# Down projection by seven half-size products instead of four quarter blocks, with operand sums made on chip

## The chip, the cores and the metric

One core of a Trainium2 chip runs the kernel. The metric is device time in microseconds (us) of one execution. TensorE multiplies, VectorE and ScalarE do elementwise work, POOL (GpSimd) issues some DMAs, SP issues the others.

## The reference, cut to what matters

One encoder layer on 512 tokens of 1024 features in float32. The change lies in the last step, with D_FF = 2816:

```python
h = rmsnorm(x, pre_ffn_w)
f = (silu(h @ w_gate) * (h @ w_up)) @ w_down
x = x + rmsnorm(f, post_ffn_w)
```

Ahead of it stand an input projection, two kinds of attention, gates and an output projection.

## The kernel before

Every float32 product is made of three matmuls. Each operand is split in a high part, which ScalarE writes by a copy into the type that TensorE reads (fp32r), and a low part, which VectorE writes as raw minus high. `mm3` (L216 to L219) issues high times high, high times low, low times high into one PSUM bank. The class `Weights` (L37 to L174) holds the list of weight units in the order of use: `load_to` (L130) issues the loads on SP's queue, five raw buffers ahead, `split_high` (L139, the copy is L147) and `split_low` (L150, the subtraction is L153) prepare a unit. Operands lie in pools: `wp` with 4 double buffers (`place_w`, L197), `up` with 18 and `up2` with 11 buffers of 128x1024.

The start (L425 to L470) is ordered by hand: `stat0` and `scale0` normalise a block of 128 tokens, `to_hT` transposes it and writes its high part on ScalarE (L339) and its low part on VectorE (L340), two weights are split, and `part` issues the first products.

The gate/up stage (L1101 to L1144) runs 20 pairs of weight units. It uses seven products of half-size blocks in place of eight: 84 matmuls of 256 columns a pair. The sums of weight blocks (S) are made on VectorE (L95 to L107), the high parts on ScalarE (L71); some low parts are made by VectorE (L76), others by ScalarE writing the negative of the high part (L73) and a DMA of POOL that adds the raw data to it (L74, "accumulate DMA" below). `ff_out` (L1031) makes the gated product, 11 tiles `F[j]` of 128x1024: two tiles of 128 hidden features, 512 tokens each.

The down projection (L1146 to L1203) walks 22 tiles of 128 hidden features. The product of a tile is 4 token blocks by 2 column halves by 3 matmuls of 512 columns, 528 in all, in eight PSUM banks. `f_split` (L1160) splits `F[j]`, `W.split_to` the weight. Up to tile 16 all eight banks are advanced together:

```python
    for k in range(KO):
        if k % 2 == 0:
            f_split()
        W.split_to(UD[k] + 4)
        for b in range(NB):
            for n in range(2):
                dn_mm(b, n, k)
```

The last six tiles then run block by block, so that a token block's norm (`scaled`, L978: square on ScalarE L982, sum on VectorE L984, power on POOL L319, weighing L987), its scale-and-add (L1200) and its output DMA (L1202) lie under the next block's matmuls. Only the last block's stand free at the end. Within these stages a scheduler sets each engine's order from the written order; engines execute their own queue in order.

## Time and profile before

| | us |
|---|---|
| median of 3 runs (lowest to highest) | 749.67 (747.67 to 749.79) |
| the profiled execution | 748.33 |
| its span in the trace | 746.6 |
| busy: TensorE, VectorE, ScalarE, POOL | 730.4, 481.1, 376.9, 82.5 |
| first and last start of the down projection's matmuls | 619.61, 739.09 |

The span runs from the first to the last event of the trace; the profiled execution's time is 1.7 us longer. Times below are from the span's start. A share of busy time is an average over stages, so it is read by stage.

### The profile page before, as it was taken

The page shows a single profiled execution, that of the slowest core. Times are in us where ns is not written, and L with a number is a line of the kernel's source. Part 1 is how long each engine was busy: PE and PEld are TensorE (multiplying, and loading weights), DVE is VectorE, ACT ScalarE, POOL GpSimd, SP SyncE. Part 2 cuts the span into 40 slices and gives each one's busy share as a digit, 9 for nine tenths or more (in the row PEclk, how much of TensorE's full clock was granted, in tenths as well). Part 3 has the DMA queues.
Part 4 walks back from the last instruction along what each step waited for, and adds up shares of the span by engine and source line. Part 5 has one row for each costly group of instructions (what it writes and reads, how often), then busy time and mean ns, then how long its engine had stood idle before and what let it go on. Part 6 is the DMA issues. An engine that isn't in the chain of part 4 may idle for free. (4 is left out here: it accounts for less than half of the span.)

```text
span 746.6 us, 11240 instructions
## 1 busy us (share of the span) xinstructions
PE 730.4 (98%) x4368; PEld 644.6 (86%) x4368; DVE 481.1 (64%) x840; ACT 376.9 (50%) x612; POOL 82.5 (11%) x129
## 2 busy tenths in 40 slices
PE   8999999999999999999999999999999999999996
PEld 7887888877888888887889999999999998888884
DVE  5625688888876633466467987777788879222333
ACT  6414565666666632453134766666666656212211
POOL 1001011122320000000011111111111110000000
PEclk9999999999999999999999999999999999999999
DMA  9436646343321213263704588878777883443112
GB/s 255 151 101 202 160 131 163 92 107 98 92 67 30 85 58 111 85 225 111 200 36 154 112 191 197 191 183 198 177 174 175 196 224 115 140 169 120 49 43 70
DMA packets 102582, 101.49 MB, mean 136 GB/s; under 512 B 3537, under 2 KB 85473, under 8 KB 102530
## 3 DMA queue, kind: packets, MB, share of 16 engines
q1 hardware_dynamic: 96080, 82.82, 38.5%
q0 software_dynamic: 6448, 17.97, 11.9%
q8 instruction: 34, 0.56, 0.3%
q14 instruction: 18, 0.15, 0.1%
q10 hardware_dynamic: 2, 0.00, 0.0%
HBM read 74.56 MB, written 4.19 MB: 105 GB/s over the span
## 5 line engine op out<-in xcount | busy, mean ns | idle before, releaser
L153 DVE TENSOR_TENSOR w<-raw,w 128x1024 fp32r<-128x1024 f32 x67 | 82.0, 1226 | 83.7 <-ACT w L147 82.6
L147 ACT ACTIVATE w<-raw 128x1024 fp32r<-128x1024 f32 x67 | 70.4, 1053 | 61.9 <-PE b L219 51.9
L217 PE MATMUL mm<-hT,w 128*128 128x512 f32 x256 | 100.8, 394 | 0.3 <-DVE v L393 0.3
L218 PE MATMUL mm<-hT,w 128*128 128x512 f32 x256 | 99.8, 390 | 0.0
L219 PE MATMUL mm<-hT,w 128*128 128x512 f32 x256 | 99.8, 390 | 0.0
L1118 PE MATMUL b<-Tl,w 128*128 128x256 f32 x240 | 66.8, 278 | 0.0
L1116 PE MATMUL b<-Th,w 128*128 128x256 f32 x240 | 66.8, 278 | 0.0
L1119 PE MATMUL b<-Th,w 128*128 128x256 f32 x240 | 66.8, 278 | 0.0
L217 PEld LDWEIGHTS mm<-hT,w 128*128 128x128 f32 x256 | 48.1, 188 | 10.3 <-DVE v L393 0.7
L219 PEld LDWEIGHTS mm<-hT,w 128*128 128x128 f32 x256 | 48.1, 188 | 10.2
L218 PEld LDWEIGHTS mm<-hT,w 128*128 128x128 f32 x256 | 48.1, 188 | 9.2
L217 PE MATMUL b<-w,fh 128*128 128x512 f32 x144 | 56.0, 389 | 0.0
L218 PE MATMUL b<-w,fh 128*128 128x512 f32 x144 | 56.0, 389 | 0.0
L219 PE MATMUL b<-w,fl 128*128 128x512 f32 x144 | 56.0, 389 | 0.0
L74 POOL DMA_DIRECT2D w<-raw x40 | 34.5, 862 | 169.2 <-ACT w L73 131.3
L1119 PE MATMUL b<-Q,w 128*128 128x256 f32 x160 | 44.5, 278 | 1.1 <-DMA w<-raw 1.1
L1119 PEld LDWEIGHTS b<-Th,w 128*128 128x128 f32 x240 | 45.4, 189 | 0.0
L1116 PEld LDWEIGHTS b<-Th,w 128*128 128x128 f32 x240 | 45.3, 189 | 0.0
L1118 PEld LDWEIGHTS b<-Tl,w 128*128 128x128 f32 x240 | 45.3, 189 | 0.0
L1118 PE MATMUL b<-Q,w 128*128 128x256 f32 x160 | 44.3, 277 | 0.0
L1116 PE MATMUL b<-Q,w 128*128 128x256 f32 x160 | 44.3, 277 | 0.0
L982 ACT ACTIVATE junk<-b 128x512 f32<-128x512 f32 x16 | 9.5, 596 | 61.6 <-PE b L219 56.8
(230 smaller groups left out, 1884.7 us busy)
## 6 DMA issues: line engine op xcount, KB each, us to landing
raw<-in_w_in_dram SPq DMA_DIRECT2D x40, 512.0 KB, 4.3
raw<-in_w_gate_dram SPq DMA_DIRECT2D x22, 512.0 KB, 4.5
raw<-in_w_up_dram SPq DMA_DIRECT2D x22, 512.0 KB, 5.1
raw<-in_w_down_dram SPq DMA_DIRECT2D x22, 512.0 KB, 3.4
w<-raw POOLq DMA_DIRECT2D x20, 512.0 KB, 6.5
K<-K SPq DMA_DIRECT2D x24, 256.0 KB, 3.2
w<-raw POOLq DMA_DIRECT2D x20, 256.0 KB, 6.2
x<-in_x_dram SPq DMA_DIRECT2D x8, 512.0 KB, 7.8
```

The costliest lines, as they stand in the source:

```text
L74: nc.gpsimd.dma_start(lo, src, accum_op=ALU.add)
L147: self.nc.scalar.activation(hi, raw, AF.Copy)
L153: (engine or self.nc.vector).tensor_sub(lo, raw, hi.bitcast(F32))
L217: nc.tensor.matmul(bank, sh, mh, start=first, stop=False)
L218: nc.tensor.matmul(bank, sh, ml, start=False, stop=False)
L219: nc.tensor.matmul(bank, sl, mh, start=False, stop=last)
L982: nc.scalar.activation(junk, bs, AF.Square, scale=1.0 / 32.0, accum_out=ss[:, n:n + 1])
L1116: nc.tensor.matmul(bank[c], sh[:, k], th[:, k], start=opens and k == 0, stop=False, **kw)
L1118: nc.tensor.matmul(bank[c], sh[:, k], tl[:, k], start=False, stop=False, **kw)
L1119: nc.tensor.matmul(bank[c], sl[:, k], th[:, k], start=False, stop=k == 3, **kw)
```

## The change

1. The 22 loaded units are now u = (h, j): two tiles of hidden features (j) and one half of the output columns (h). All j run for h = 0 (pass 0), then for h = 1 (pass 1), there in the order 5 to 10, 0 to 4: the gated product's operands of j = 5 to 10 are kept, those of 0 to 4 prepared again.
2. Each unit's block product is made by seven half-size products (P1 to P7) of sums of blocks: S of the gated product, T of the weight. Each has 2 token blocks by 3 matmuls of 256 columns: 42 a unit, 924 in all, into seven banks.
3. New preparation per unit. Weight: ScalarE writes the high part and its negative (768 columns each), POOL issues an accumulate DMA of 384 KB, all two units ahead; VectorE makes T (512 + 256 + 256), ScalarE its high part, VectorE its low part (1024). Gated product (16 times): ScalarE the high part of 768; its low part is VectorE's for even j, and for odd j ScalarE's negative with an accumulate DMA; VectorE makes S (4 x 256), ScalarE its high part, VectorE its low part.
4. At the end of pass 0 the seven banks are combined (ScalarE once, VectorE seven times, L1303 to L1314) while pass 1 begins; squares and weighing of that half follow in unit 11.
5. At the end of pass 1 the last two units' products stand together, P3 and P2 by halves of their token blocks, each followed by combine, squares, power, weighing (L1331) and scale-and-add with its output DMA (`give`, L1336 and L1338).
6. At the start the first weight's high part is written by VectorE, ahead of the first `to_hT`.

The core of the diff (line numbers L1100 and up in the order rows below are those of the changed file; `product` is L1283 to L1290, `combine` L1296 to L1314):

```diff
@@ -131,8 +132,13 @@
         while self.n_dma < min(n, len(self.units)):
             src, shape, _ = self.units[self.n_dma]
             raw = self.raw_pool.tile([128, 1024], F32, tag="raw", name="raw")
-            view = raw.rearrange("p (a b) -> p a b", a=shape[0])
-            self.nc.sync.dma_start(view, src)
+            if len(shape) == 3:
+                view = raw.rearrange("p (a b c) -> p a b c", a=shape[0], b=shape[1])
+                for a in range(shape[0]):
+                    self.nc.sync.dma_start(view[:, a], src[:, a])
+            else:
+                view = raw.rearrange("p (a b) -> p a b", a=shape[0])
+                self.nc.sync.dma_start(view, src)
...
+    ORDER_D = [(0, j) for j in range(KF // 2)]
+    ORDER_D += [(1, j) for j in (*range(KEEP, KF // 2), *range(KEEP))]
+    UD = [W.add(dram(w_down, 256 * j * D + 512 * h,
+                     [[D, 128], [256, 2], [128 * D, 2], [1, 256]]), (2, 2, 256), None)
+          for h, j in ORDER_D]
...
     stat0(1)
+    W.split_high(nc.vector)
     to_hT(hh, 0, hT, ps_s, "s")
     hh = scale0(1)
-    for _ in range(2):
-        W.split_high()
+    W.split_high()
     W.split_low()
...
+        def a0():
+            f = F[j].rearrange("p a t -> p (a t)")
+            st["f"] = f
+            st["lo"] = low_slots(j, turn)
+            hi, lo = U(F32R, [128, 1024], "fh"), st["lo"][0]
+            nc.scalar.activation(hi[:, :768], f[:, :768], AF.Copy)
+            if j % 2:
+                nc.scalar.activation(lo[:, :768], hi[:, :768].bitcast(F32), AF.Copy, scale=-1.0)
+                nc.gpsimd.dma_start(lo[:, :768], f[:, :768], accum_op=ALU.add)
+            else:
+                nc.vector.tensor_sub(lo[:, :768], f[:, :768], hi[:, :768].bitcast(F32))
+            keep(hi, lo, "A12", "A22", "A11")
+        def s1():
+            f = st["f"]
+            a12, a22, a11, a21 = (f[:, 256 * i:256 * i + 256] for i in range(4))
+            S = st["S"] = U(F32, [128, 1024], "S")
+            nc.vector.tensor_add(S[:, 0:256], a21, a22)
+            nc.vector.tensor_sub(S[:, 256:512], S[:, 0:256], a11)
+            nc.vector.tensor_sub(S[:, 512:768], a21, a11)
+            nc.vector.tensor_sub(S[:, 768:], a12, S[:, 256:512])
+        def s2():
+            hi, lo = U(F32R, [128, 1024], "fh"), st["lo"][1]
+            nc.scalar.activation(hi, st["S"], AF.Copy)
+            nc.vector.tensor_sub(lo, st["S"], hi.bitcast(F32))
+            keep(hi, lo, "S1", "S2", "S3", "S4")
+            fop[j] = out
+        return [a0, s1, s2]
...
+        def d0():
+            W.load_to(UD[u] + 1)
+            raw = st["r"] = W.raws.pop(UD[u])
+            if u % 3 == 2:
+                hi, lo = U(F32R, [128, 1024], "dh"), U(F32R, [128, 1024], "dl")
+            else:
+                hi, lo = place_w(16, 1040)
+            nc.scalar.activation(hi[:, :768], raw[:, :768], AF.Copy)
+            nc.scalar.activation(lo[:, :768], hi[:, :768].bitcast(F32), AF.Copy, scale=-1.0)
+            nc.gpsimd.dma_start(lo[:, :768], raw[:, :768], accum_op=ALU.add)
+            keep(hi, lo, "B21", "B11", "B22")
+            W.n_split += 1
+            W.load_to(W.n_split + W.raw_bufs)
...
+        def d1():
+            raw = st["r"]
+            T = st["T"] = U(F32, [128, 1024], "T")
+            b12 = raw[:, 768:].unsqueeze(1).to_broadcast([128, 2, 256])
+            nc.vector.tensor_sub(T[:, :512].rearrange("p (a b) -> p a b", a=2), b12,
+                                 raw[:, 256:768].rearrange("p (a b) -> p a b", a=2))
+            nc.vector.tensor_sub(T[:, 512:768], raw[:, 512:768], T[:, 0:256])
+            nc.vector.tensor_sub(T[:, 768:], raw[:, 0:256], T[:, 512:768])
+        def d2():
+            if u == NU - 1:
+                hi, lo = U(F32R, [128, 1024], "dh"), U(F32R, [128, 1024], "dl")
+            else:
+                hi, lo = place_w(16, 1040)
+            nc.scalar.activation(hi, st["T"], AF.Copy)
+            nc.vector.tensor_sub(lo, st["T"], hi.bitcast(F32))
+            keep(hi, lo, "T1", "T3", "T2", "T4")
+            wop[u] = out
+        return [d0, d1, d2]
...
+    def down_steps(u):
+        if u >= NU:
+            return []
+        h, j = ORDER_D[u]
+        d = dw[u]
+        f = f_steps(j, h) if h == 0 or j < KEEP else []
+        return f[:1] + [d[1], d[2]] + f[1:]
...
-        nxt = steps_of(n + 1)
+        last_pair = n == len(pairs) - 1
+        nxt = [dw[0][0]] + down_steps(0) if last_pair else steps_of(n + 1)
...
+    PRODS = (("P1", "A11", "B11"), ("P6", "S2", "T2"), ("P5", "S1", "T1"), ("P7", "S3", "T3"),
+             ("P4", "A22", "T4"), ("P3", "S4", "B22"), ("P2", "A12", "B21"))
+    PLAIN_LAST = tuple(PRODS[i] for i in (1, 2, 3, 4, 0, 5, 6))
...
+        (ah, al), (bh, bl) = fop[ORDER_D[u][1]][an], wop[u][bn]
+        for i in halves:
+            o, c = banks[nm][:, 256 * i:256 * i + 256], slice(128 * i, 128 * i + 128)
+            nc.tensor.matmul(o, ah[:, c], bh, start=first and i == 0, stop=False,
+                             skip_group_check=True)
+            nc.tensor.matmul(o, ah[:, c], bl, start=False, stop=False, skip_group_check=True)
+            nc.tensor.matmul(o, al[:, c], bh, start=False, stop=last, skip_group_check=True)
...
+    def combine(nm, h, pv, halves=(0, 1)):
+        i = slice(halves[0], halves[-1] + 1)
+        bank = two(banks[nm])[:, i]
+        q = [two(t)[:, i] for t in pv]
+        if nm == "P1":
+            nc.scalar.activation(q[0], bank, AF.Copy)
+        elif nm == "P6":
+            nc.vector.tensor_add(q[1], q[0], bank)
+        elif nm == "P5":
+            nc.vector.tensor_add(q[2], q[1], bank)
+        elif nm == "P7":
+            nc.vector.tensor_add(ysum[1, h][:, i, 256:], q[2], bank)
+            nc.vector.tensor_add(q[3], q[1], bank)
+        elif nm == "P4":
+            nc.vector.tensor_add(ysum[1, h][:, i, :256], q[3], bank)
+        elif nm == "P3":
+            nc.vector.tensor_add(ysum[0, h][:, i, 256:], q[2], bank)
+        else:
+            nc.vector.tensor_add(ysum[0, h][:, i, :256], q[0], bank)
...
+    def give(r, i, h):
+        b = 2 * r + i
+        y, c = ysum[r, h][:, i], slice(512 * h, 512 * h + 512)
+        nc.vector.scalar_tensor_tensor(y, y, ss3[r, i][:, 3:4], x2[b][:, c],
+                                       op0=ALU.mult, op1=ALU.add)
+        nc.sync.dma_start(dram(out, 16 * b * D + 512 * h,
+                               [[D, 16], [64 * D, 8], [1, 512]]), y)
...
+    dw[1][0]()
     x2 = []
...
+    for u in range(NU - 2):
+        h, j = ORDER_D[u]
+        end = u == HALF - 1
+        nxt = down_steps(u + 1) + ([dw[u + 2][0]] if u + 2 < NU else [])
+        if u + 2 < NU:
+            nxt = nxt[-1:] + nxt[:-1]
+        if u == NU - 3:
+            nxt += down_steps(NU - 1)
+        first = u % HALF == 0
+        if end:
+            for r in range(2):
+                ysum[r, 0] = U(F32, [128, 2, 512], "y3", up2)
+            pv = [t for _ in range(2) for t in halves_of(U(F32, [128, 1024], "pv"))]
+        for p in (PRODS if end else PLAIN_LAST):
+            product(u, p, first, end)
+            if end:
+                combine(p[0], 0, pv)
+            if nxt:
+                nxt.pop(0)()
+        for fn in nxt:
+            fn()
+        if end:
+            banks.clear()
+        if u == HALF:
+            pow_ = U(F32, [128, D], "pow", up2)
+            nc.sync.dma_start(pow_, bcast(post_ffn_w, D))
+            for r in range(2):
+                for i in range(2):
+                    squares(r, i, 0)
+            for r in range(2):
+                for i in range(2):
+                    weigh(r, i, 0)
...
+    for p in PRODS[:5]:
+        for u in (NU - 2, NU - 1):
+            product(u, p, False, u == NU - 1)
+        combine(p[0], 1, pv)
+    for i in range(2):
+        squares(1, i, 1)
+        rstd(1, i)
+        weigh(1, i, 1)
+    for i in range(2):
+        for p in PRODS[5:]:
+            for u in (NU - 2, NU - 1):
+                product(u, p, False, u == NU - 1, (i,))
+            combine(p[0], 1, pv, (i,))
+        squares(0, i, 1)
+        rstd(0, i)
+        weigh(0, i, 1)
+        if i == 0:
+            for q in range(2):
+                for h in range(2):
+                    give(1, q, h)
+        for h in range(2):
+            give(0, i, h)
```

VectorE in the down projection. Before, it has two kinds of rows (`fl` and `w` are low parts of the gated product and of a weight):

```order
L153 TENSOR_TENSOR w<-raw,w 128x1024
L1165 TENSOR_TENSOR fl<-f,fh 128x1024 x4
L153 TENSOR_TENSOR w<-raw,w 128x1024 x4
L1165 TENSOR_TENSOR fl<-f,fh 128x1024
L153 TENSOR_TENSOR w<-raw,w 128x1024 x7
```

After, one even unit of pass 0:

```order
L1187 TENSOR_TENSOR T<-raw 128x512
L1138 TENSOR_TENSOR fl<-f,fh 128x768
L1189 TENSOR_TENSOR T<-raw,T 128x256
L1145 TENSOR_TENSOR S<-f 128x256
L1190 TENSOR_TENSOR T<-raw,T 128x256
L1146 TENSOR_TENSOR S<-S,f 128x256
L1147 TENSOR_TENSOR S<-f 128x256
L1148 TENSOR_TENSOR S<-f,S 128x256
L1198 TENSOR_TENSOR w<-T,w 128x1024
L1153 TENSOR_TENSOR fl<-S,fh 128x1024
```

One low part for a weight unit and half of one for the gated product became seven sums and two or three low parts; an odd unit has all but L1138, and in pass 1 units 11 to 16 have only T's rows.

TensorE, the first matmuls of unit 3 (j = 3, odd; `fl_6333` is A's low part made by ScalarE and the accumulate DMA):

```order
L1287 MATMUL b_6359<-w_6394,fh_6474 128x256 [waits Activation_49]
L1289 MATMUL b_6359<-w_6394,fh_6474 128x256 [waits DMASW3_49]
...
L1287 MATMUL b_6310<-w_6494,fh_6514 128x256 [waits Activation_49]
...
L1289 MATMUL b_6310<-w_6494,fh_6514 128x256 [waits DVE_49]
...
L1290 MATMUL b_6349<-w_6494,fl_6333 128x256 [waits DMASW5_49]
L1287 MATMUL b_6349<-w_6494,fh_6474 128x256
```

The wait on DMASW5 is for the accumulate DMA (L1136) of this unit; it and the 29 matmuls behind it are 30 of the unit's 42.

The end, VectorE, before (the last token block), and after from the first half of P3 on (`ss_7135` and `ss_7138` belong to the two halves of the tokens that finish last):

```order
L987 TENSOR_TENSOR y_6971<-b,pow 128x512
L984 TENSOR_SCALAR ss_6972<-ss_6972 128x1
L987 TENSOR_TENSOR y_6971<-b,pow 128x512
L1200 SCALAR_TENSOR_TENSOR y_6971<-y_6971,ss_6972,x_6819 128x512 x2
```

```order
L1314 TENSOR_TENSOR y_7662<-pv,b 128x256
L1336 SCALAR_TENSOR_TENSOR y_7003<-y_7003,ss_7141,x_7442 128x512
L1336 SCALAR_TENSOR_TENSOR y_7663<-y_7663,ss_7141,x_7442 128x512
L1325 TENSOR_SCALAR ss_7135<-ss_7135 128x1
L1331 TENSOR_TENSOR y_7662<-y_7662,pow 128x512
...
L1336 SCALAR_TENSOR_TENSOR y_7662<-y_7662,ss_7135,x_7438 128x512
L1312 TENSOR_TENSOR y_7662<-pv,b 128x256
L1314 TENSOR_TENSOR y_7662<-pv,b 128x256
L1325 TENSOR_SCALAR ss_7138<-ss_7138 128x1
L1331 TENSOR_TENSOR y_7662<-y_7662,pow 128x512
L1336 SCALAR_TENSOR_TENSOR y_7002<-y_7002,ss_7138,x_7440 128x512
```

Five rows for the last block became a row of some 25 for all four, with the second half's combine (the second L1312 and L1314) behind six L1336. On TensorE the second half's first matmul waits for the first half's L1312.

## Rows read from the trace of the kernel before

**Rows 1.** The page, part 1: busy time, share and instructions of each engine.

```profile
PE 730.4 (98%) x4368; PEld 644.6 (86%) x4368; DVE 481.1 (64%) x840; ACT 376.9 (50%) x612; POOL 82.5 (11%) x129
```

**Rows 2.** Windows: stretch, us, busy PE, PEld, DVE, ACT, POOL, clock, DMA, GB/s.

```profile
540.00:560.00 20.00, 19.93 (x173) 19.73 (x172) 15.96 (x25) 13.08 (x18) 3.81 (x5) 1.00 0.77 179
640.00:650.00 10.00, 10.00 (x45) 8.26 (x44) 2.45 (x2) 3.07 (x3) 0.00 (x0) 1.00 0.44 150
```

**Rows 3.** Waits in the down projection: us in total, times, longest.

```profile
ACT w L147 <- PE b L219: 48.6, 13, 4.4
```

**Rows 4.** Timeline of TensorE: start, duration, line; gate/up stage, then down projection.

```profile
594.51 0.28 PE L1116 MATMUL b<-Th,Q 128*128 128x256 f32 x1
...
598.95 0.28 PE L1116 MATMUL b<-Th,w 128*128 128x256 f32 x1
...
619.61 0.40 PE L217 MATMUL b<-w,fh 128*128 128x512 f32 x1
...
739.09 0.39 PE L219 MATMUL b<-whi,fl 128*128 128x512 f32 x1
```

**Rows 5.** Timeline of VectorE in the gate/up stage.

```profile
603.71 0.69 DVE L96 TENSOR_TENSOR S<-S,raw 128x512 f32<-128x512 f32 x1
604.31 0.41 DVE L1124 TENSOR_TENSOR pv<-pv,b 128x256 f32<-128x256 f32 x1
604.64 0.69 DVE L107 TENSOR_TENSOR S<-raw,S 128x512 f32<-128x512 f32 x1
...
605.57 1.22 DVE L76 TENSOR_TENSOR w<-S,w 128x1024 fp32r<-128x1024 f32 x1
606.71 0.41 DVE L1128 TENSOR_TENSOR G<-pv,b 128x256 f32<-128x256 f32 x1
```

**Rows 6.** Timeline of ScalarE in the gate/up stage.

```profile
604.43 1.06 ACT L71 ACTIVATE w<-S 128x1024 fp32r<-128x1024 f32 x1 [2.44 <-DVE S L96]
605.39 1.04 ACT L147 ACTIVATE w<-raw 128x1024 fp32r<-128x1024 f32 x1
...
608.29 0.62 ACT L73 ACTIVATE w<-w 128x512 fp32r<-128x512 f32 x1
608.81 0.37 ACT L1134 ACTIVATE G<-b 128x256 f32<-128x256 f32 x1
```

**Rows 7.** POOL's accumulate DMAs of L74, gate/up stage: instructions, then time to landing.

```profile
L74 POOL DMA_DIRECT2D w<-raw x39: 853/860/872, 419.5 to 609.2; - x39
...
DMA to landing us min/median/max: 4.4/6.4/8.9
```

**Rows 8.** The page, part 5: weight loads of the gate/up stage (busy us, mean ns).

```profile
L1116 PEld LDWEIGHTS b<-Th,w 128*128 128x128 f32 x240 | 45.3, 189 | 0.0
```

**Rows 9.** Timeline of the end, after the last matmul.

```profile
739.57 0.60 ACT L982 ACTIVATE junk<-b 128x512 f32<-128x512 f32 x1 [3.37 <-PE b L219]
...
740.29 0.21 DVE L984 TENSOR_SCALAR ss<-ss 128x1 f32<-128x1 f32 x1 [3.37 <-ACT junk L982]
...
740.65 0.54 POOL L319 TENSOR_TENSOR ss<-ss,mhalf 128x1 f32<-128x1 f32 x1 [7.62 <-DVE ss L984]
741.23 1.42 DVE L1200 SCALAR_TENSOR_TENSOR y<-y,ss,x 128x512 f32<-128x512 f32 x2
```

**Rows 10.** The start: first weight's load, then the timelines of VectorE, ScalarE and TensorE.

```profile
L135 SPq DMA_DIRECT2D raw<-in_w_in_dram x1: 596/596/596, 2.1 to 2.1; - x1
...
DMA to landing us min/median/max: 7.1/7.1/7.1
...
10.81 1.44 DVE L340 TENSOR_TENSOR hT<-tb,hT 128x512 fp32r<-128x512 f32 x2 [1.49 <-ACT hT L339]
...
11.42 2.94 ACT L147 ACTIVATE whi<-raw 128x1024 fp32r<-128x1024 f32 x3
...
12.53 1.20 PE L397 MATMUL mm<-whi,hT 128*128 128x512 f32 x4 [1.63 <-ACT whi L147]
```

**Rows 11.** Windows at the span's end, columns as in rows 2.

```profile
743.00:744.00 1.00, 0.00 (x0) 0.00 (x0) 0.00 (x0) 0.00 (x0) 0.00 (x0) 1.00 0.73 166
744.00:745.00 1.00, 0.00 (x0) 0.00 (x0) 0.00 (x0) 0.00 (x0) 0.00 (x0) 0.76 0.98 348
745.00:746.60 1.60, 0.00 (x0) 0.00 (x0) 0.00 (x0) 0.00 (x0) 0.00 (x0) 0.50 0.02 6
```

More of the change, by code (lines that the diff above doesn't have):

```diff
@@ L26 @@
 UB = 18
+KEEP = 5
 WIN = ((0, 192), (64, 248), (192, 248), (320, 192))
@@ L1089, in block_kernel, with low_slots @@
     ff_out(G, Uu)
+    low = {}
+    def low_slots(j, turn):
+        n = {0: {1: 0, 2: 1, 3: 2, 4: 3, 5: 0, 6: 1, 7: 2, 8: 3},
+             1: {0: 0, 1: 1, 2: 2, 3: 3}}[turn].get(j)
+        if n is None:
+            pool = up if (turn, j) == (0, 0) else up2
+            return U(F32R, [128, 1024], "fl", pool), U(F32R, [128, 1024], "fl", pool)
+        if not low:
+            for q in range(2):
+                low[q] = hp.tile([128, 4160], F32R, tag="hT", name="fl")
+        t, c = low[n // 2], 32 + 2048 * (n % 2)
+        return t[:, c:c + 1024], t[:, c + 1024:c + 2048]
@@ new lines, in block_kernel, with f_steps, keep @@
+    fop, wop = {}, {}
+    def f_steps(j, turn):
+        st, out = {}, {}
+        def keep(hi, lo, *names):
+            for i, nm in enumerate(names):
+                c = slice(256 * i, 256 * i + 256)
+                out[nm] = hi[:, c], lo[:, c]
+        def a0():
[25 more added lines that the diff above has]
+        return [a0, s1, s2]
@@ new lines, in w_steps, with keep @@
+    def w_steps(u):
+        st, out = {}, {}
+        def keep(hi, lo, *names):
+            for i, nm in enumerate(names):
+                c = slice(256 * i, 256 * i + 256)
+                out[nm] = hi[:, c], lo[:, c]
+        def d0():
+            assert W.n_split == UD[u], (W.n_split, UD[u])
+            W.load_to(UD[u] + 1)
[28 more added lines that the diff above has]
+        return [d0, d1, d2]
@@ L1093, in block_kernel @@
+    NU = len(UD)
+    def down_steps(u):
[5 more added lines that the diff above has]
+        return f[:1] + [d[1], d[2]] + f[1:]
+    dw = [w_steps(u) for u in range(NU)]
     ORDER = (("A11", "B11", "A", "p"), ("S2", "T2", "B", "v"), ("S1", "T1", "C", "v5"),
@@ new lines, in block_kernel, with product @@
+    PLAIN_LAST = tuple(PRODS[i] for i in (1, 2, 3, 4, 0, 5, 6))
+    banks = {}
+    ysum, ss3 = {}, {}
+    def product(u, p, first, last, halves=(0, 1)):
+        nm, an, bn = p
+        if nm not in banks:
+            banks[nm] = psB.tile([128, 512], F32, tag="b", name="b")
+        (ah, al), (bh, bl) = fop[ORDER_D[u][1]][an], wop[u][bn]
[5 more added lines that the diff above has]
+            nc.tensor.matmul(o, al[:, c], bh, start=False, stop=last, skip_group_check=True)
@@ new lines, in squares, with rstd @@
+    def squares(r, i, h):
+        if (r, i) not in ss3:
+            ss3[r, i] = sp.tile([128, 4], F32, tag="ss3", name="ss3")
+        junk = U(F32, [128, 512], "junk")
+        nc.scalar.activation(junk, ysum[r, h][:, i], AF.Square, scale=1.0 / 32.0,
+                             accum_out=ss3[r, i][:, h:h + 1])
+    def rstd(r, i):
+        ss = ss3[r, i]
+        nc.vector.tensor_scalar(ss[:, 2:3], ss[:, 0:1], ss[:, 1:2], EPS,
+                                op0=ALU.add, op1=ALU.add)
+        rms_r(ss[:, 2:3], ss[:, 3:4])
@@ new lines, in halves_of @@
+    def halves_of(t):
+        return t[:, :512], t[:, 512:]
+    HALF = KF // 2
+    dw[1][0]()
+    x2 = []
+    for u in range(NU - 2):
[30 more added lines that the diff above has]
+                    weigh(r, i, 0)
+        if u == NU - 6:
+            for b in range(NB):
+                t = U(F32, [128, D], "x2", up2)
+                nc.sync.dma_start(t, x2d[b])
+                x2.append(t)
```

67 lines of the change are left out of this document (10 added, 57 removed).

## The prediction

> **What bounds the kernel now.** I read the page's busy shares first [rows 1]: TensorE is busy for 730.4 of 746.6 us, VectorE for 481.1 and ScalarE for 376.9. So before, the only thing to win is columns streamed on TensorE. Then the busy time by stretches [rows 2], because an average hides that the cover is uneven. In the gate/up stage, which already uses seven products, VectorE is busy 15.96 of 20 us. In the down projection it is busy 2.45 of 10 and ScalarE 3.07, with TensorE at 10.00 of 10. There the preparing engines wait for TensorE, not the other way round [rows 3]: ScalarE's splits waited 48.6 us for matmuls to give buffers back. The question is whether seven products, which put the gate/up stage's kind of load on VectorE, still leave TensorE first.
>
> The prices come from the timelines. In a busy engine I take the step from one start to the next, since the printed duration overlaps the next instruction's start. TensorE [rows 4]: 40 matmuls of 256 columns start from 594.51 to 598.95, so 39 steps of 0.1138. The 528 matmuls of 512 columns start from 619.61 to 739.09: 527 steps of 0.2267, ending at 739.48. VectorE [rows 5]: 0.60 for 512 columns (603.71 to 604.31), 0.33 for 256 (604.31 to 604.64), 1.14 for 1024 (605.57 to 606.71); for 768 I interpolate 0.87. ScalarE [rows 6]: 0.96 for 1024 (604.43 to 605.39), 0.52 for 512 (608.29 to 608.81), 0.74 estimated for 768. When another engine waits for the result I take the duration (1.06, and 0.84 for 768) instead. An accumulate DMA of POOL [rows 7] lands 6.4 us after its issue, 4.4 at best and 8.9 at worst.
>
> **Columns.** 22 units of 42 matmuls are 924 x 0.1138 = 105.2 us; the old stage streamed 528 x 0.2267 = 119.7. Gain **-14.5**. This holds if weight loads stay hidden though their number rises by 396. They do in the gate/up stage: a load takes 0.188 to 0.189 [rows 8] and the matmuls still follow each other at 0.1138. The Trainium skill ("TensorE: Matmul & The Clock Gate", Part 3, The mechanism) says that a load is pulled ahead when its row group does not conflict or it goes to the background buffer; were these full-array loads to conflict, each would stand on the path.
>
> **Pass 0.** VectorE's new work for a unit: sums of weights 0.60 + 0.33 + 0.33 = 1.26, sums of the gated product 4 x 0.33 = 1.32, two low parts of 1024 columns 2.28, together 4.86. Even units also have the low part of 768 columns, 0.87: 5.73. Two units make 10.6, where TensorE needs 2 x 4.78 = 9.56. So VectorE no longer fits beneath TensorE: that alone is 1.0 us per two units. VectorE also stands still when it reaches a low part and ScalarE's copy is not there: the T copy (1.06) starts only when T is complete, and the S copy follows on the same engine, with a 768 copy for the unit two ahead between or after. I work that out at 0.5 us in an odd unit and 0.6 to 1.0 in an even one, about 12.4 us per two units.
>
> The odd units have a longer chain. ScalarE makes the high part and the negative (1.7 us) only after the T copy, a weight copy, the S copy and the weight's negative (1.06 + 0.74 + 1.06 + 0.74), which follow VectorE's T, complete 2.6 us after it starts the even unit. That is about 9.1 us with the waits; then POOL issues the accumulate DMA, landing 6.4 later, and 30 of the unit's 42 matmuls stand behind the first that reads it (3.4 us). Step by step: unit 0 can begin at 620.9, since its S copy waits for sums that stand behind a low part in VectorE's queue, and ends at 625.7. VectorE is through with it at 622.15. Unit 1's accumulate, issued after four ScalarE copies from 620.9, lands at 630.5, so TensorE stands for 4.1 us from 626.35; unit 1 ends at 634.75. Later landings come at 644.6, 656.9, 668.4 and 681.0 for units 3, 5, 7 and 9; unit 9 ends at 684.3 and unit 10 at 689.1. At full rate from 619.6 it would be 672.0, so pass 0 costs **+17.1**. Its lower bound goes by VectorE's busy time alone: from 622.15, 1.47 for the last operations of the gate/up stage in front, 10 units with 52.95, and 1.9 of matmuls behind the last low part is 678.4, so +6.4.
>
> On the accumulate's landing the Trainium skill ("DMA: Bandwidth & Descriptors", Anatomy of one DMA) fits 2.0 us plus the bytes over 436 GB/s for POOL's path: an estimate of 2.9 us for 384 KB, half of what the rows show. By it the odd units would be ready 3.5 us sooner and the sum would come out near 761. The trace decides, since its 6.4 [rows 7] is the same kind of DMA between the same two pools; the bounds are its 4.4 and 8.9, which is -4 to +5 at the two places where a landing counts (the odd units of pass 0 as a constant lag, and unit 20).
>
> **Between the passes.** Seven combines of 0.6 come onto VectorE. Unit 11's T is copied by ScalarE behind the first of them (+0.9) and its low part stands behind another sum and combine (+0.8): **+1.7**, bounds 0 and 2.5. The squares and weighing of pass 0 lie in unit 11, where a unit costs VectorE only 1.26 + 1.14: free, as long as VectorE is not the bound there.
>
> **Pass 1.** For six units only T is new, 2.4 us of VectorE under 4.78 of TensorE: near nothing. The last five units prepare A again: three even, two odd. Unit 20 (j=3) waits for its accumulate until about 740.5, with 70 matmuls of units 20 and 21 behind; small waits before it and S's low part of unit 21 come on top. **+5.8**; without unit 20's wait 2.8.
>
> **The tail.** Before [rows 9]: the last matmul ends at 739.48, ScalarE's square starts at 739.57, VectorE's sum at 740.29, POOL's power at 740.65, and two scale-and-adds at 741.23 end at 742.65: 3.3 us after TensorE's work would be streamed (I take 739.32), then 3.95 for DMA and end. After: the reduced S of unit 21 lets P6, P5 and P7 finish together, so six combines start only then (five of 0.60 and a half one of 0.33, less the 1.0 of matmuls beside them: 2.4 us after the last matmul of the first token half). The second half's products wait for the first half's combine of the same bank, and that half's combine stands in VectorE's queue behind two sums, two weighings, and two, then four scale-and-adds (0.67 each) with another sum and weighing between: 10.6 us after that matmul. Then square, sum, power, weigh and two scale-and-adds as before, 3.3 us. Last VectorE end 13.9 us after that matmul, which is 12.4 after the point where the remaining 12 matmuls (1.4 us) would have streamed out. **+9.1** (12.4 - 3.3); bounds +7 (combines hidden) and +11.
>
> **The start.** The first weight lands 7.1 us after 2.1 [rows 10]. VectorE copies it at about 9.3 to 10.5, before the low part at 10.81. ScalarE's split at 11.42 (three of 2.94, so the first ends near 12.4) held the first real matmul, at 12.53. ScalarE loses one copy and hT's low part, ending at 12.25, becomes the next limit: **-0.7**, bounds -1.0 and +0.3 (VectorE's copy delaying the low part).
>
> **Sum.** -14.5 + 17.1 + 1.7 + 5.8 + 9.1 - 0.7 = +18.5. The profiled execution took 748.33, so 766.8, **767 us**. The median of the runs shown, 749.67, is 1.3 above the profiled one, well inside the range. A change of 0.3%, 2.2 us, is about what a measurement of this kernel tells from none.
>
> **Rivals.** (1) VectorE's busy time alone is the limit: ScalarE's copies and the landings fit beneath. For it: ScalarE's own work for two units, 4 x 0.96 + 7 x 0.74 = 9.0 us, fits beneath VectorE's 10.6. Pass 0 +6.4, boundary +0.9, pass 1 +2.8: -14.5 + 6.4 + 0.9 + 2.8 + 9.1 - 0.7 = +4.0, **752**. Against: queues are in order, and the copies wait for the sums of the same unit.
> (2) Faster: VectorE keeps pace. It decides at 9.56 us for two units. Then pass 0 costs unit 0's 1.2 only, the boundary and pass 1 nothing: -14.5 + 1.2 + 9.1 - 0.7 = -4.9, **743**. For it: VectorE is idle for a fifth of the gate/up stage [rows 2]. Against: 10.6 by the rows, and the order prepares one unit ahead only.
> (3) TensorE's clock falls in the stalls. In the trace the granted clock is still 1.00 up to 744 and 0.50 (1.2 of 2.4 GHz) from 745 [rows 11], and 0.76 in between, so it fell some 5 us after the last matmul. My longest stall is 4.1 us. With two units streamed at half rate, 2 x 4.78 more: +28, **776**.
> (4) The weight loads set the rate: 924 x 0.188 = 173.7 instead of 105.2: **835**. The rows speak against it [rows 4, 8].
>
> **How the numbers follow.** Forecast 0.62 (by its bounds 760 to 773), rival 1 0.17, rival 2 0.05, rival 3 0.14, rival 4 0.02. The range 754 to 778 holds the forecast, most of rival 3 and the upper part of rival 1. Faster by over 0.3%: rival 2, 0.05. Within: the lower end of rival 1, 0.05. Slower: 0.90.
>
> **What would show it.** In the changed profile: matmuls of 0.114 in the down stage; TensorE busy well under 9 of 10 in pass 0, its idle time ended by POOL's accumulate of the gated product or VectorE's low parts; VectorE near 85% there, near half in pass 1; some 17 us from TensorE's first long gap at the end to the span's end; the first real matmul 0.5 to 1 us earlier. The forecast is wrong if pass 0 takes under 60 us (I have 69.5) or the tail's last VectorE operation comes under 9 us after the first half's last matmul.

## The result and the profile after

| | before | after |
|---|---|---|
| median, lowest to highest, us | 749.73 (747.67 to 749.94, 4 runs) | 782.12 (778.36 to 783.13, 4 runs) |
| profiled execution, span, us | 748.33, 746.6 | 783.13, 781.4 |
| mean granted clock of TensorE | 0.999 | 0.973 |

The change makes the kernel 1.0437 times as long, 95% interval 1.0411 to 1.0462: 32 us slower, where 17 were forecast. Slower was right, the size was not, and 782 lies above the range (754 to 778).

The page's busy times of the changed kernel, which answer to [rows 1]:

```profile
PE 743.4 (95%) x4764; PEld 669.6 (86%) x4764; DVE 554.2 (71%) x1001; ACT 434.2 (56%) x685; POOL 109.3 (14%) x158
```

TensorE is busy longer than before though it streams fewer columns, and its share fell. Its timeline (start, duration, line; in brackets the idle time before and what ended it): the down projection's first matmul, the long stalls of pass 0, and the wait near the end.

```profile
625.40 0.38 PE L1287 MATMUL b<-w,fh 128*128 128x256 f32 x1
...
631.41 0.28 PE L1287 MATMUL b<-w,fh 128*128 128x256 f32 x1
634.74 0.58 PE L1290 MATMUL b<-w,fl 128*128 128x256 f32 x1 [3.05 <-DMA fl<-f]
...
651.08 0.58 PE L1290 MATMUL b<-w,fl 128*128 128x256 f32 x1 [1.95 <-DMA fl<-f]
...
667.26 0.58 PE L1290 MATMUL b<-w,fl 128*128 128x256 f32 x1 [3.17 <-DMA fl<-f]
...
691.39 0.58 PE L1290 MATMUL b<-w,fl 128*128 128x256 f32 x1 [1.91 <-DMA fl<-f]
...
766.18 0.55 PE L1287 MATMUL b<-dh,fh 128*128 128x256 f32 x1 [3.03 <-DVE y L1312]
```

Two things stand out. The stage begins at 625.40, where it began at 619.61 before [rows 4]: 5.8 us are lost in code that the change hardly touches. And behind each stall the matmuls take 0.4 to 0.6 us instead of 0.28. The windows (columns as in [rows 2]) show why:

```profile
632.50:633.00 0.50, 0.00 (x0) 0.00 (x0) 0.50 (x1) 0.50 (x1) 0.00 (x0) 1.00 1.12 172
633.00:633.50 0.50, 0.00 (x0) 0.00 (x0) 0.50 (x1) 0.50 (x2) 0.03 (x1) 0.63 0.82 193
633.50:634.00 0.50, 0.00 (x0) 0.00 (x0) 0.50 (x2) 0.42 (x1) 0.50 (x1) 0.50 1.14 305
...
639.50:640.00 0.50, 0.50 (x4) 0.50 (x4) 0.00 (x0) 0.00 (x0) 0.00 (x0) 0.55 0.15 51
640.00:640.50 0.50, 0.50 (x7) 0.50 (x6) 0.00 (x0) 0.00 (x0) 0.00 (x0) 1.00 0.04 14
```

The granted clock falls to 0.50 (1.2 of 2.4 GHz) while TensorE stands, near 633.1, 1.4 us after the last matmul's end at 631.7, and is 1.00 again only near 640, 5 us after the matmuls go on. The other three long stalls of pass 0 have a fall too:

```profile
650.00:650.50 0.50, 0.00 (x0) 0.00 (x0) 0.50 (x3) 0.33 (x1) 0.50 (x1) 0.69 0.76 174
...
667.00:667.50 0.50, 0.24 (x1) 0.24 (x2) 0.50 (x1) 0.50 (x2) 0.00 (x0) 0.76 1.32 147
...
691.00:691.50 0.50, 0.11 (x1) 0.11 (x1) 0.50 (x1) 0.00 (x0) 0.50 (x1) 0.65 1.09 381
```

By the share of 0.50 in each window the falls lie near 650.2, 667.3 and 691.2, which is 1.1, 3.2 and 1.7 us after a last matmul's end. In all, TensorE streams for 17.7 us of pass 0 at half its clock. In the last two windows of the first stall (639.5 to 640.5) VectorE and ScalarE are idle too. What they wait for stands in their timelines:

```profile
640.90 0.85 ACT L1176 ACTIVATE w<-raw 128x768 fp32r<-128x768 f32 x1 [3.57 <-PE b L1290]
641.66 1.04 ACT L1152 ACTIVATE fh<-S 128x1024 fp32r<-128x1024 f32 x1
...
642.73 1.23 DVE L1153 TENSOR_TENSOR fl<-S,fh 128x1024 fp32r<-128x1024 f32 x1 [4.14 <-ACT fh L1152]
```

ScalarE's next weight copy waits for a buffer that the slow matmuls still read; the copy of S stands behind it in ScalarE's queue, and VectorE, the busiest of the preparing engines, waits 4.14 us for that. So a stall slows TensorE, and slow TensorE delays the preparation that ends the next stall.

The end, VectorE, which answers to [rows 9]:

```profile
762.20 0.69 DVE L1303 TENSOR_TENSOR pv<-pv,b 128x512 f32<-128x512 f32 x1 [1.05 <-PE b L1290]
...
765.71 0.41 DVE L1312 TENSOR_TENSOR y<-pv,b 128x256 f32<-128x256 f32 x1
...
773.06 0.41 DVE L1312 TENSOR_TENSOR y<-pv,b 128x256 f32<-128x256 f32 x1
773.39 0.41 DVE L1314 TENSOR_TENSOR y<-pv,b 128x256 f32<-128x256 f32 x1
...
775.91 1.41 DVE L1336 SCALAR_TENSOR_TENSOR y<-y,ss,x 128x512 f32<-128x512 f32 x2 [0.44 <-POOL ss L327]
```

The second half's combine stands 7.4 us behind the first's, as the order said, and the last VectorE instruction ends at 777.3.

### The profile page after: what moved, and what is told of

The parts are those of the page before. It is cut to its first block, busy times and chain, and to the rows that moved or that the text cites. A ratio compares the mean times of both kernels' runs of the same rounds, so it can differ in the third digit from the quotient of the medians.

```text
span 781.4 us, 12448 instructions
## 1 busy us (share of the span) xinstructions
PE 743.4 (95%) x4764; PEld 669.6 (86%) x4764; DVE 554.2 (71%) x1001; ACT 434.2 (56%) x685; POOL 109.3 (14%) x158
## 5 line engine op out<-in xcount | busy, mean ns | idle before, releaser
L223 PE MATMUL mm<-hT,w 128*128 128x512 f32 x256 | 101.9, 398 | 0.3 <-DVE v L401 0.3
L224 PE MATMUL mm<-hT,w 128*128 128x512 f32 x256 | 101.0, 395 | 0.0
L225 PE MATMUL mm<-hT,w 128*128 128x512 f32 x256 | 101.0, 395 | 0.0
L159 DVE TENSOR_TENSOR w<-raw,w 128x1024 fp32r<-128x1024 f32 x49 | 60.0, 1226 | 43.3 <-ACT w L153 43.0
L1290 PE MATMUL b<-w,fl 128*128 128x256 f32 x258 | 70.3, 307 | 10.4 <-DMA fl<-f 10.1
L1287 PE MATMUL b<-w,fh 128*128 128x256 f32 x258 | 70.2, 297 | 2.0 <-ACT fh L1152 1.3
L1289 PE MATMUL b<-w,fh 128*128 128x256 f32 x258 | 70.7, 296 | 0.8 <-DVE w L1198 0.5
L1290 PEld LDWEIGHTS b<-w,fl 128*128 128x128 f32 x258 | 50.8, 213 | 11.4 <-DMA fl<-f 10.9
L153 ACT ACTIVATE w<-raw 128x1024 fp32r<-128x1024 f32 x49 | 51.4, 1052 | 12.6 <-PE mm L405 7.7
L225 PEld LDWEIGHTS mm<-hT,w 128*128 128x128 f32 x256 | 48.0, 187 | 11.7
L1287 PEld LDWEIGHTS b<-w,fh 128*128 128x128 f32 x258 | 50.4, 204 | 3.3 <-ACT fh L1152 2.1
L1289 PEld LDWEIGHTS b<-w,fh 128*128 128x128 f32 x258 | 50.5, 203 | 1.3 <-DVE w L1198 0.7
L1245 PE MATMUL b<-Q,w 128*128 128x256 f32 x160 | 45.1, 282 | 0.6 <-DMA w<-raw 0.6
L1242 PE MATMUL b<-Q,w 128*128 128x256 f32 x160 | 45.2, 283 | 0.0
L1245 PEld LDWEIGHTS b<-Th,w 128*128 128x128 f32 x240 | 45.2, 188 | 0.0
```

The source lines that it names most:

```text
L153: self.nc.scalar.activation(hi, raw, AF.Copy)
L159: (engine or self.nc.vector).tensor_sub(lo, raw, hi.bitcast(F32))
L223: nc.tensor.matmul(bank, sh, mh, start=first, stop=False)
L224: nc.tensor.matmul(bank, sh, ml, start=False, stop=False)
L225: nc.tensor.matmul(bank, sl, mh, start=False, stop=last)
L1242: nc.tensor.matmul(bank[c], sh[:, k], th[:, k], start=opens and k == 0, stop=False, **kw)
```

## The experiments

Theories at the start: **place** (the new kind of small tile grows the statistics pool by 192 bytes per partition, moves the pools behind it, and matmuls that read them go slower), **clock** (as above), **landing** or **VectorE** (what sets the pace of pass 0), **tail**. "Pass 0" below is the time from the down projection's first matmul to the start of pass 0's last combine on VectorE: 80.4 us in the change. The forecast's pass 0 ends earlier, with unit 10's last matmul: 68.2 us there (620.9 to 689.1), 76.2 in the change. The kernel before was run again beside each group of runs. Its medians were 749.8, 747.9 and 748.1 us; ratios are to the one of the same group, and a difference between medians of two groups is uncertain by about 2 us.

**The place alone, on the kernel before.** One unused tile:

```diff
+    sp.tile([128, 4], F32, tag="ss3", name="ss3")
     banks = [psB.tile([128, 512], F32, tag="b", name="b") for _ in range(8)]
```

> The kernel before with nothing added but one unused small tile of a new kind in the pool of small statistics, as the change has one: that pool grows by 192 bytes per partition, and the pools behind it (hT with the transposed operands and Q, up2, the attention's) move from addresses that are a multiple of 128 bytes to ones that leave 64. Theory (place): this alone is what makes the changed kernel reach the down projection 5.8 us late instead of 0.7 early; the first matmul of the down projection starts at 626 (before 619.6), the matmuls of 256 columns that read Q follow each other at 0.118 to 0.119 instead of 0.113, and the time is 6 to 9 us above the kernel before. Rival (start): the earlier start shifts the loads against the work and the middle loses by that; then this kernel is within 1 us of before.

Measured 756.22 us (756.09 to 758.24), ratio 1.0092 (1.0074 to 1.0111). Its timeline of TensorE: a run of 12 matmuls that read Q, and the down projection's first.

```profile
590.96 0.28 PE L1116 MATMUL b<-Th,Q 128*128 128x256 f32 x1
...
592.27 0.28 PE L1119 MATMUL b<-Th,Q 128*128 128x256 f32 x1
...
626.57 0.40 PE L217 MATMUL b<-w,fh 128*128 128x512 f32 x1
```

11 steps in 1.31 us are 0.119 each. The same run in the kernel before takes 1.24 (0.113):

```profile
584.49 0.28 PE L1116 MATMUL b<-Th,Q 128*128 128x256 f32 x1
...
585.73 0.28 PE L1119 MATMUL b<-Th,Q 128*128 128x256 f32 x1
```

The changed kernel shows 1.31 too:

```profile
589.66 0.28 PE L1242 MATMUL b<-Th,Q 128*128 128x256 f32 x1
...
590.97 0.28 PE L1245 MATMUL b<-Th,Q 128*128 128x256 f32 x1
```

The order of the instructions on VectorE, ScalarE and POOL is the same as before, and TensorE's waits ahead of the down projection did not grow (4.1 us against 5.2): a 192-byte move of the pools behind costs 6 to 7 us. Place holds.

**The changed kernel with its pools in the old place.**

```diff
-            ss3[r, i] = sp.tile([128, 4], F32, tag="ss3", name="ss3")
+            ss3[r, i] = sp.tile([128, 4], F32, tag="ss2", name="ss3")
```

> The changed kernel with its statistics tiles of a kind that the pool already has, so that no pool moves; the order of all instructions is the same. Theory (place): the first matmul of the down projection starts at 618 to 619.5 (changed kernel 625.4), and the time is 7 to 11 us below the changed kernel's 782.1, 771 to 775. Rival: 782, as changed.

Measured 772.45 (771.48 to 773.75), ratio 1.0298 (1.0279 to 1.0318): 9.7 us below the change. Its down projection begins at

```profile
617.90 0.38 PE L1287 MATMUL b<-w,fh 128*128 128x256 f32 x1 [0.17 <-ACT fh L1152]
```

7.5 us earlier than in the change; the other 2 lie in the down projection, where pass 0 is 77.2 instead of 80.4. The nine traces of this kernel and its variants below begin the down projection between 617.9 and 620.1, and they are apart by nearly as much already 100 us into the trace. So the place costs 5.3 to 7.5 us ahead of the down projection, and this trace is at the upper end. All further variants of the changed kernel start from this one.

**The start alone, on the kernel before** (`W.split_high(nc.vector)` ahead of the first `to_hT`, one `W.split_high()` less behind it).

> The kernel before with the first weight's high part on VectorE ahead of the first transposes, nothing else. Forecast's step: -0.7 us (bounds -1.0 to +0.3). The changed kernel's trace shows -1.2 at 40 us and only -0.2 left at 240 us: by the theory that the rest was lost to the moved addresses, this kernel keeps -1.0 to -1.3 to the end (748.5). Rival: the start's gain is given back at later waits that do not depend on it (attention waits for ScalarE and VectorE): -0.3 to +0.3. Rival (start): the middle drifts as in the changed kernel: +5.

Measured 747.36 (746.93 to 747.44) beside 749.82 of before, ratio 0.9966 (0.9953 to 0.9979). The down projection begins at

```profile
618.25 0.40 PE L217 MATMUL b<-w,fh 128*128 128x512 f32 x1
```

which is 1.4 us earlier than before (span 745.2 beside 746.6), but traces of one and the same beginning differ by 2.2 us, so the gain rests on the ratio: 0.3%, with an interval clear of 1. Of the two parts that were tried alone, place and start, this is the one that gains, and this kernel is faster than both.

**Whether any move by a multiple of 128 bytes is safe** (b_vec with two more unused tiles, 384 bytes).

> b_vec (747.4) with two unused tiles in the statistics pool: the pools behind it move by 384 bytes per partition, from addresses that leave 128 to ones that leave 0 on division by 256, and stay multiples of 128. Theory (the step of 128 is what matters): within 1 us of b_vec, 746.4 to 748.4, and the matmuls that read Q still follow each other at 0.113. Rival (256, or any move costs): 2 to 7 us away.

Measured 752.56 (752.23 to 753.46), ratio 1.0057 (1.0039 to 1.0075): 5 us slower than b_vec by the medians of two groups, 7 by the ratios. The theory's second half fell. The first product of the down projection:

```profile
623.93 0.40 PE L219 MATMUL b<-w,fh 128*128 128x512 f32 x1
```

Here the runs of Th with Q take 1.25 us as before; other pairs of operands lost. By the mean step between starts, Q with w takes 0.118 instead of 0.115, and hT with w (512 columns) 0.233 instead of 0.228. So it isn't a pool's own address on a grid of 128 bytes; that it is the position of the two operands to each other would fit all three kernels, but was not tried by itself.

**The clock.** In the odd units of pass 0, filling matmuls into an unused bank ahead of the one that waits:

```diff
+            if u < 10 and u % 2 and nm == "P4" and i == 0:
+                if "idle" not in banks:
+                    banks["idle"] = psB.tile([128, 512], F32, tag="b", name="idle")
+                for _ in range(FILLS):
+                    nc.tensor.matmul(banks["idle"][:, :256], ah[:, c], bh, start=True, stop=True,
+                                     skip_group_check=True)
```

> As a_place, and 30 matmuls of 256 columns into an unused bank stand on TensorE's queue ahead of the matmul that waits for the accumulate DMA, in units 1, 3, 5, 7 and 9 of pass 0: they fill the stalls (3.4 us each) without touching the results. Theory (clock): in pass 0 the granted clock fell to 0.50 in or behind four stalls of 2.5 to 3.5 us, and the slow stretches hold buffers that ScalarE waits for; with the stalls filled the clock stays at 1.00 in pass 0 and the time is 6 to 10 us below a_place, although 150 matmuls are added. Rival: preparation is the limit all the same and the clock costs nothing: within 2 us of a_place, or up to 10 above it where the filling is longer than the stall.

> As a_fill (769.6) with 20 filling matmuls instead of 30 in each odd unit of pass 0. With 30, TensorE was busy in 5.00 of 5 us throughout pass 0, so 84 + 30 matmuls at 0.114 = 13.0 us set the pace of two units and not the preparation. Theory: with 20 the pace is the preparation's, 12.4 by the forecast, or 104 x 0.114 = 11.8 if that is longer: 3 us shorter in pass 0, 766 to 767.5. Rival: preparation takes 13 us for two units by itself; then stalls of about 1 us come back and the time stays at 769 to 770, or rises if the clock falls.

With 30: 769.64 (769.39 to 770.37), ratio 1.0267 (1.0251 to 1.0283). With 20: 766.09 (765.08 to 766.39), ratio 1.0234 (1.0212 to 1.0257). 100 matmuls that compute nothing make the kernel 6.4 us faster than a_place by the medians of two groups, 4.8 by the ratios. Windows over the whole of pass 0, a_place, then 20 fillings (its pass 0 and 1.3 us more):

```profile
617.90:695.00 77.10, 64.41 (x485) 62.39 (x486) 64.00 (x109) 51.89 (x61) 14.71 (x17) 0.91 0.78 166
```

```profile
620.10:691.00 70.90, 70.75 (x595) 69.52 (x596) 65.13 (x112) 52.07 (x63) 14.71 (x17) 1.00 0.85 186
```

VectorE and ScalarE do the same work, 64 and 52 us, but in 71 us instead of 77: VectorE's share goes from 0.83 to 0.92, since it no longer pauses for slow matmuls. Pass 0 is 69.6 us with 20 fillings, 74.6 with 30 (where TensorE itself was the limit, as the second expectation had it), 77.2 with none. To the end of unit 10 it is 67.2 with 20, near the forecast's 68.2, which was a pass 0 at full clock. But with 20 TensorE is busy 70.75 of 70.90 us as well, and two units take 11.7 us, about the 104 x 0.114 of their matmuls: what the preparation alone needs at full clock isn't shown, only that it is no more than that. The first expectation's 6 to 10 us came at most with 20, not with 30 (2.8 us).

**Landing or VectorE.** Two ways to take the accumulate DMA out of the way. In a_dve VectorE makes the low part in odd units too (`if j % 2` never true); in a_lead2 odd units are prepared two units ahead (`LEADS` names them):

```diff
+    def lead(u):
+        h, j = ORDER_D[u]
+        if (h == 0 or j < KEEP) and j % 2 and u in LEADS:
+            fst[u] = f_steps(j, h)
+            return fst[u][:1]
+        return []
...
-        nxt = down_steps(u + 1) + ([dw[u + 2][0]] if u + 2 < NU else [])
+        nxt = down_steps(u + 1)
...
-            nxt = nxt[-1:] + nxt[:-1]
+            nxt = lead(u + 2) + nxt + [dw[u + 2][0]]
```

The last lines do one thing more: the weight's copy and accumulate for two units ahead (`dw[u + 2][0]`) stood first in a unit and now stand last.

> As a_place, but the low part of 768 columns of the gated product is VectorE's in every unit (before: in even ones; odd ones used ScalarE's negative and an accumulate DMA). VectorE gets 7 x 0.87 = 6 us more work, ScalarE 7 x 0.85 less, seven DMAs go. Theory (landing): as the landing was what ended the stalls, pass 0 gets shorter although VectorE works more: two units cost 11.5 of VectorE's time and 13 with its waits, no stall is longer than 2 us, the clock stays at 1.00 in most of pass 0: 765 to 770. Rival (VectorE is the limit): 5 units x 0.87 more in pass 0 and up to 2 in pass 1: 775 to 779.

> As a_place, but the part of the gated product that needs an accumulate DMA (odd j: ScalarE's high part and negative, POOL's DMA) is prepared two units ahead instead of one, in units 1, 3, 5, 7, 9, 18 and 20; no work is added. Theory (landing): TensorE's long stalls of pass 0 end with that DMA's landing, because it is issued last; issued a unit earlier it lands before it is read, the stalls that it ends go, and what is left is VectorE's pace of 12 to 12.4 us per two units: pass 0 66 to 70 us instead of 77, the stall of 2 us at unit 20 gone, 761 to 766 in all (a_place 772.5). Rival (VectorE and ScalarE): the queue of sums and copies is the limit and the landing only ends last; then the stalls end with VectorE's low parts instead and the time stays within 3 us of 772.5.

Measured 772.32 (771.72 to 772.57) and 771.45 (771.32 to 772.43): both beside a_place's 772.45, though pass 0 fell to 72.9 and 72.0 us. Both expectations (765 to 770, 761 to 766) missed. In a_dve the long stalls are gone, the clock stays at 1.00 in pass 0, VectorE is busy 0.93 of the time, and TensorE's waits (8.4 us up to unit 10's end) end with ScalarE's copies and VectorE's low parts:

```profile
640.00:660.00 20.00, 17.42 (x137) 16.12 (x136) 18.68 (x33) 13.73 (x17) 2.85 (x4) 1.00 0.60 138
```

In a_lead2 TensorE's waits up to 691 us went to the weights' accumulate DMAs, which the edit itself had moved back (us in total, times, longest):

```profile
PE b L1302 <- DMA dl<-raw: 5.5, 3, 2.2
PE b L1302 <- DMA w<-raw: 4.2, 4, 1.7
```

Of the 4.2 and 5.2 us won in pass 0 the spans keep 2.0 and 1.3 (769.9 and 770.6 beside a_place's 772.0, the longest of its four). Both begin the down projection 0.6 and 0.9 us later, and pass 1 gives back the rest. In a_dve units 18 and 20 cost VectorE more. In a_lead2 it is a wait that neither the forecast nor the experiments had in view, VectorE's for the load of the norm's weights (`pow`), which unit 11's weighing reads:

```profile
723.33 2.49 DVE L1344 TENSOR_TENSOR y<-y,pow 128x512 f32<-128x512 f32 x4 [6.41 <-DMA pow<-in_post_ffn_w_dram]
729.04 0.58 PE L1300 MATMUL b<-w,fh 128*128 128x256 f32 x1 [4.27 <-ACT fh L1153]
```

The load was issued at 714.5 and landed 8.8 us later; the sums of S stand behind the weighing in VectorE's queue, ScalarE's copy of S behind them, and TensorE waits 4.3 us for that copy. The change itself and a_place have no such wait, a_dve has 0.5 us of it and 20 fillings have 2.6. So in pass 0 the landing is worth 4 to 5 us, and what it would be worth in all with that load issued earlier was not tried. Behind the landing the preparation takes 12.7 us for two units in a_dve.

a_lead3, the early preparation in pass 0 alone:

> As a_lead2 (771.5), with the early preparation in pass 0 alone (units 1, 3, 5, 7 and 9), units 18 and 20 as in the change. a_lead2's trace has pass 0 some 4 us shorter than a_place and a new wait of 4.6 us in pass 1 (ScalarE's copy of S at unit 17 or 18) where the early units' work is in front. Theory: without it the 4 us of pass 0 remain: 767 to 769. Rival: the time gained in pass 0 goes at the next wait behind it in any case: 771 to 772.5.

Measured 770.96, from 768.55 to 773.61: inconclusive. Its profiled execution (773.61) has pass 0 at 72.6; then VectorE waits 4.2 us for `pow`, and TensorE 2.2 us for the copy of S behind that and 2.5 for the accumulate of unit 20.

**Less work on VectorE.** The four sums of S on POOL, in a_place and in a_dve (`nc.gpsimd` for `nc.vector` in `s1`):

> As a_place (772.5), with the four sums of the gated product (S, 4 x 0.33 us of VectorE in each unit that makes them) on POOL instead of VectorE. Theory (VectorE's occupancy): two units cost VectorE 10.6 - 2.6 = 8.0 us, less than TensorE's 9.6, and pass 0 is no longer VectorE's: 62 to 68 us instead of 77, 757 to 764 in all. Rival 1 (landing): the accumulate DMA of the odd units still lands last and the long stalls stay: 768 or more. Rival 2: POOL's sums take several times VectorE's 0.4 us, or slow VectorE, and S comes later than before: above 775.

> As a_dve (772.3: VectorE makes all low parts of the gated product, no accumulate DMA for it), with S on POOL as in a_pool. Theory (VectorE's occupancy): a_dve's VectorE was busy 9.2 to 9.5 of 10 us in pass 0, 13 us per two units; with 2.6 less it is 8.8 of work per two units, and TensorE's 9.6 becomes the limit again but for short waits: pass 0 56 to 62 us instead of 72, 756 to 762 in all. Rival: POOL's sums come too late or slow VectorE: 770 or more.

Measured 787.07 (786.47 to 787.97) and 790.71 (789.93 to 791.97): slower by 15 and 18 us. Rival 2, and more of it than expected. Groups of instructions between 618 and 700 us on VectorE (busy, mean ns) and from 600 on POOL, a_pool:

```profile
L1187 DVE TENSOR_TENSOR T<-raw 128x512 f32<-128x512 f32 x12 | 21.0, 1749 | 0.0
L1153 DVE TENSOR_TENSOR fl<-S,fh 128x1024 fp32r<-128x1024 f32 x11 | 17.8, 1621 | 2.5 <-ACT fh L1152 2.4
...
L1145 POOL TENSOR_TENSOR S<-f 128x256 f32<-128x256 f32 x16 | 18.1, 1131 | 1.8 <-PE b L1289 1.8
```

The same groups of VectorE in a_place:

```profile
L1153 DVE TENSOR_TENSOR fl<-S,fh 128x1024 fp32r<-128x1024 f32 x11 | 13.4, 1221 | 6.1 <-ACT fh L1152 6.1
L1187 DVE TENSOR_TENSOR T<-raw 128x512 f32<-128x512 f32 x14 | 9.5, 684 | 0.0
```

A sum of 256 columns takes POOL 1.13 us (VectorE 0.42), and VectorE's own instructions take 1749 ns instead of 684 and 1621 instead of 1221 in the mean. The means mix two kinds: with no sum on POOL beside it an instruction takes its usual time, with sums beside it it takes several times that.

```profile
639.20 0.68 DVE L1187 TENSOR_TENSOR T<-raw 128x512 f32<-128x512 f32 x1
...
644.25 5.26 DVE L1187 TENSOR_TENSOR T<-raw 128x512 f32<-128x512 f32 x1
```

```profile
644.46 1.04 POOL L1146 TENSOR_TENSOR S<-S,f 128x256 f32<-128x256 f32 x1
...
649.03 1.06 POOL L1148 TENSOR_TENSOR S<-f,S 128x256 f32<-128x256 f32 x1
```

The work came off VectorE by the count, not by the time, so these two runs don't tell how fast pass 0 would be with a lighter VectorE; that stays open.

**The tail.** P3 and P2 unsplit, their combines ahead of all scale-and-adds:

```diff
-    for i in range(2):
-        for p in PRODS[5:]:
-            for u in (NU - 2, NU - 1):
-                product(u, p, False, u == NU - 1, (i,))
-            combine(p[0], 1, pv, (i,))
+    for p in PRODS[5:]:
+        for u in (NU - 2, NU - 1):
+            product(u, p, False, u == NU - 1)
+        combine(p[0], 1, pv)
...
```

> As a_place, but the last two products are not split by token halves: their combines come before all eight scale-and-adds. Theory (tail): the second half's combine no longer stands behind six scale-and-adds of the first half, and the wait of TensorE for a bank at the end (3.3 and 1.1 us) goes; VectorE's own row of about 25 operations stays, so the end comes 1.5 to 2.5 us sooner: 770 to 771. Rival: VectorE's work alone sets the end and nothing moves: within 0.5 us of 772.5.

Measured 773.63, from 768.21 to 776.08: inconclusive by time. The trace tells what happened (VectorE):

```profile
752.12 1.23 DVE L1153 TENSOR_TENSOR fl<-S,fh 128x1024 fp32r<-128x1024 f32 x1 [1.12 <-ACT fh L1152]
756.19 0.69 DVE L1303 TENSOR_TENSOR pv<-pv,b 128x512 f32<-128x512 f32 x1 [2.84 <-PE b L1290]
...
765.39 4.06 DVE L1336 SCALAR_TENSOR_TENSOR y<-y,ss,x 128x512 f32<-128x512 f32 x6
```

From the first combine (756.19) to VectorE's end (769.45) it is 13.3 us, in a_place 15.1: the 1.8 that were expected. But the first combine comes 4.1 us after the last low part, in a_place 2.1, as more matmuls stand ahead of it now (36 instead of 16 start between the two). Gain and loss cancel: 17.3 us from that low part to the end, 17.2 in a_place.

## Why the forecast was right in sign and wrong in size

The profiled execution's span is 16.3 us above the forecast's 765.1 (746.6 + 18.5). By stretches:

- **Up to the first product of the down projection:** 620.2 forecast, 625.4 measured, +5.2. The first step that failed is one that the forecast did not have: it took the stages before as untouched but for the start, so their term stood at nothing. The pools' place cost 5.3 to 7.5 us there (change against the kernels in the old place). The start's -0.7 was too small: b_vec's ratio makes it -2.5 (0.9966 of 749.8; by its interval -1.6 to -3.5).
- **Pass 0, to unit 10's last matmul:** 68.2 forecast, 76.2 measured, +8.0. The mechanism was right: the stalls end with the odd units' accumulate, at 3.05, 1.95, 3.17 and 1.91 us near or below the 4.1 I had as the longest, and the DMAs landed as the rows of before said:

```profile
DMA to landing us min/median/max: 5.6/5.8/8.8
```

(the change's L1136, 384 KB; an estimate of 2.9 us by the Trainium skill's fit, "DMA: Bandwidth & Descriptors", Anatomy of one DMA: measurement decides.) The second step that failed is rival 3: "it fell some 5 us after the last matmul. My longest stall is 4.1 us", with a chance of 0.14. One fall of the clock, at the program's end, was taken for how long TensorE may stand; in the change it fell 1.1 to 3.2 us after a last matmul, in four stalls. Its price: 4.8 to 6.4 us (a_place to 20 fillings), 9.56 in the rival; half of the 17.7 us streamed at half clock would be 8.9 in the change, and a_place's 12.1 would be 6.0. The place cost 3 more in this pass. In a_place the waits for the accumulate were, in us in total, times and longest,

```profile
PE b L1290 <- DMA fl<-f: 10.5, 5, 3.4
```

and 2.3 went to copies and low parts, where the forecast's pass 0 holds 15.6 us beyond its 462 matmuls: the waits were priced a little high, and the clock at nothing. Two readings of the forecast are off without effect: 619.6 and 462 x 0.1138 make 672.2, not 672.0, so its +17.1 is 16.9; and the accumulate of the gated product (`fl<-f`) does not run between the pools of the rows it was priced by (`w<-raw`).
- **From there through pass 1, to the last matmul before the wait for a bank:** 701.56 to 762.87, 61.3 us; 58.9 forecast. The wait for unit 20's accumulate is there, at 2.0 us; some 1.8 are the slower steps of the moved place.
- **Tail:** from the last matmul before the bank wait (762.87) to VectorE's end 14.45 us, 13.9 forecast; then 4.0 to the end, 3.95 forecast.
- **Columns:** 0.1138 a matmul was right for the place of before (a_place: 0.115 in pass 1, the mean step between starts without the stalls), in the moved place it was 0.118.

With the clock held and the old place (20 fillings) the kernel takes 766.1, and its stretches are 620.1, 67.2, 58.9, 14.4 and 4.0 us beside the forecast's 620.2, 68.2, 58.9, 13.9 and 3.95. The forecast's 767 was for that kernel. That it comes so near in pass 0 is in part luck: there the fillings stand on TensorE where the forecast had waits, and the forecast's pace of 12.4 us for two units was not met (11.7 with the fillings, 12.7 in a_dve).

Rival 1 (752) and rival 2 (743) fell with a_dve: without landing and at full clock, pass 0 still took 68.5 us to the end of unit 10, with VectorE at 18.7 of 20; rival 1's sum has 57.5 there, and a_dve's own addition to VectorE is only 5 x 0.87. The weight loads (rival 4) stayed hidden. The measured time as three terms: 766.1 with the clock held and the old place, 6.4 for the clock, 9.7 for the place (by the ratios 17.5 above before, 4.8 and 10.4). They add up to 782.1 because they are differences of the same medians; what supports them is the trace of each.

## What to carry to other kernels

Before a change takes columns off TensorE, add up what the preparing engines must do for the columns that are left. Here that was more than TensorE's time (VectorE alone 10.6 against 9.6 us for two units), and the saving became stalls; whether a lighter VectorE would have cured it stays open. A stall can halve TensorE's clock for longer than it lasted (3.05 us of standing, 5 us of slow matmuls behind it). Filling matmuls gained more (4.8 to 6.4 us) than the two ways tried to take the landing away (within 2 us of a_place). Where an earlier stage gets faster, look at what the next one loads: one late load of norm weights held VectorE for up to 6.4 us. A new tile in a small pool can move every pool behind it: compare addresses when stages that nobody edited get slower. And try a bundle's parts alone: here the smallest part, one copy on another engine at the start, is the only one that was found to gain.
